# The third mixer's inverse: substitution on 16x16 blocks, the rest by products on TensorE

## The chip, the cores and the metric

The kernel runs on one core of a Trainium2 chip. The metric is the device time of one execution in microseconds. The profile is of one execution, and its times are in microseconds unless marked ns. Engines: PE is TensorE, DVE VectorE, ACT ScalarE, POOL GpSimd, SP SyncE, which issues most DMAs. A name such as `SPq` is an engine's queue of DMA issues.

## The reference

Two layers of a diffusion backbone, each with three mixers side by side (a gated linear attention, a windowed attention and an RWKV-7 time mixing), a merge through sigmoid gates, and a feed-forward part. The change is in the third mixer, which runs this recurrence in both directions of time:

```python
def rwkv7_scan(r, w, k, v, kk, a, s0, with_out):
    def step(S, inp):
        w_t, k_t, v_t, kk_t, a_t = inp[:5]
        sa = jnp.einsum('bhvk,bhk->bhv', S, kk_t)
        S = S * w_t[:, :, None, :] - sa[..., None] * (kk_t * a_t)[:, :, None, :] + v_t[..., None] * k_t[:, :, None, :]
        return S, jnp.einsum('bhvk,bhk->bhv', S, inp[5])
    s_fin, y = lax.scan(step, s0, xs)
```

Eight heads of 64 channels, 768 tokens, in fp32. Taken over a block of 32 tokens, the terms with `kk` make a unit triangular system of 32x32 for each head, whose inverse turns the block's inputs into its updates of the state.

## The kernel before

The class `Rwkv` has two lanes: f runs forward in time, b backward. Each takes six groups of 128 tokens, four blocks of 32 each. A group has two parts. Its **front** is `prep` (decay sums; the products `xp` of keys and updates, which a mask turns into the tile `X` on DVE, L1507; the products `bk` transposed by PE into `tp` and copied to `bkt` on ACT, L1518 and L1519) and then `inverse`. Its **chain** is four steps, one for each block: `yp` on PE (L1576, L1581), negated into `ysb` on ACT (L1586), `up` = inverse times `ysb` on PE (L1596), copied to `uv` on ACT (L1604), `sp` on PE, and the new state `sblk` on DVE (L1617); POOL scales the old state into `scf` or `scb` meanwhile (L1590). The output `op` (L1602, L1622) stands beside it.

`inverse` takes 32 triangular systems at once (4 pairs of heads x 2 heads x 4 blocks), four copies of each, so that 128 partitions hold 8 of the 32 rows each. The triangles go from `X` to DRAM (`d1`, two DMAs, L1530) and come back broadcast as `L` of 128 x 32 x 32 (L1532). `G` starts as an identity from DRAM (`gid`, on ACT's queue, L1537). 31 steps of substitution follow, each a product into `ftmp` (L1548) and a subtraction from `G` (L1549), in lane f on DVE and in lane b on POOL. `G` goes to DRAM (`d2`, four DMAs, L1553) and comes back as `TT` (L1555), which `up` reads.

The two lanes take turns, and before each half step of a chain two steps of the next group's front are issued. In layer 0 the fronts run one group ahead (`ahead`), in layer 1 two. In between, GEMM jobs of other parts fill PE: `px` and `pz` (three products of fp32 halves `hh`, `hl` with `wh`, `wl`; `wh` is made on ACT, L71, and `wl` on DVE, L72). In layer 0 they are spread by the number of turns, in layer 1 paced by the chain's hops. The order on each engine is set by the Tile scheduler from the program as written; every engine works its list in that order. The PSUM tag "a" with two buffers is shared by `xp`, `tp` and, later, `gp` and `ty`.

Of the kernel before, what the change touches and what calls it, by code (L numbers as in the profile page):

```python
# [1216 lines left out]
class Rwkv:  # L1217
# [43 lines left out]
    def open(self):  # L1261
# [13 lines left out]
        self.masks = ld("rmask", [128, 2, 64], I["rmask"])  # L1275
        self.smask = P.tile([128, 16, 34], F32, name="smask")
# [3 lines left out]
        for d in "fb":  # L1280
            self.sc[d] = P.tile([128, 4, 64], F32, name=f"sc{d}")
            t = P.tile([128, 4, 128], F32, name=f"sblk{d}")
            nc.gpsimd.memset(t, 0.0)
            self.sb[d] = t

# [236 lines left out]
    def inverse(self, d, g, later):  # L1522

        nc, T = self.nc, self.T
        d1 = self.D.tile([2, 16, 32, 32], F32, name="d1", tag="d1", bufs=3)
        d2 = self.D.tile([8, 4, 32, 32], F32, name="d2", tag="d2", bufs=3)
        X = self.hs[d, g]["X"]
        for q in range(2):
            r0 = 0 if q == 0 else 96
            nc.sync.dma_start(d1[q].rearrange("u j i -> j u i"), X[r0:r0 + 32].rearrange("j e w p i -> j (e w p) i")[:, :, 0:32])  # L1530
        L = T.tile([128, 32, 32], F32, name="L", tag="L", bufs=2)
        nc.sync.dma_start(L.rearrange("u j i -> u (j i)"), d1.rearrange("q u j i -> (q u) (j i)").unsqueeze(1).to_broadcast([32, 4, 1024]))  # L1532
# [3 lines left out]
        G = T.tile([128, 8, 32], F32, name="G", tag="G", bufs=2)  # L1536
        nc.scalar.dma_start(G, self.I["gid"])  # L1537
        tmp = T.tile([128, 128], F32, name="ftmp", tag="ftmp", bufs=2)
        eng = nc.vector if d == "f" else nc.gpsimd
        for n in range(31):  # L1540
            if d == "f":
                j, rows, cols = n, slice(0, n // 4 + 1), slice(n + 1, 32)
            else:
                j = 31 - n
                rows, cols = slice(j // 4, 8), slice(0, j)
            a, m = rows.stop - rows.start, cols.stop - cols.start
            t = tmp[:, 0:a * m].rearrange("q (a b) -> q a b", b=m)
            eng.tensor_tensor(out=t, in0=G[:, rows, j:j + 1].to_broadcast([128, a, m]), in1=L[:, j:j + 1, cols].to_broadcast([128, a, m]), op=ALU.mult)  # L1548
            eng.tensor_tensor(out=G[:, rows, cols], in0=G[:, rows, cols], in1=t, op=ALU.subtract)  # L1549
            if n % 8 == 7:  # L1550
                yield
        for s in range(4):
            nc.sync.dma_start(d2.rearrange("m p (a s) i -> s (m p) a i", s=4)[s], G[s::4])  # L1553
# [180 lines left out]
def _consts():  # L1734
    f = np.float32
# [145 lines left out]
```

## Time and profile before

| | |
|---|---|
| median of 3 runs (lowest, highest) | 3249.8 us (3247.38, 3262.34) |
| the profiled execution's own time | 3250.64 us |
| its span | 3248.8 us |
| PE busy | 2975.4 us, 92% of the span |
| DVE busy | 1735.5 us, 53% |
| ACT busy | 1126.6 us, 35% |
| POOL busy | 951.7 us, 29% |

The span is the part of the profiled execution between its first and its last instruction; 1.8 us of that execution lie around it. Busy time is an average over parts with different limits, and the third mixer's recurrence fills two stretches of the span: about 660 to 1100 us in layer 0 and 2340 to 2760 us in layer 1. Waits name the engine and line whose end let the waiting one go on. The granted clock is the share of full speed that TensorE was given.

### The profile page before, as it was taken

Reading aid. Unit: us, or ns where it says so; the run is one execution under the profiler, and the core shown is the slowest. Engines: PE = TensorE matmul, PEld = TensorE weight load, DVE = VectorE, ACT = ScalarE, POOL = GpSimd, SP = SyncE. Lnnn points to the kernel's source line nnn. Section 1 sums busy time; section 2 is a strip of 40 time slices with the busy share of each in tenths; the row PEclk is TensorE's granted clock in tenths of the full one; section 3 lists DMA queues with packets and bytes.
Section 4 is the critical chain, followed back from the end, with each engine's and each line's share of the span. In section 5 each row is a group of like instructions: output and inputs, shape, how many; then the busy total and the mean of one; then the engine's idle time right before and its main releaser. Section 6 shows DMA issues by size and latency. Waiting matters only on the chain. (4 is left out here: it accounts for less than half of the span.)

```text
span 3248.8 us, 62663 instructions
## 1 busy us (share of the span) xinstructions
PE 2975.4 (92%) x25760; PEld 2376.0 (73%) x25760; DVE 1735.5 (53%) x3336; ACT 1126.6 (35%) x2226; POOL 951.7 (29%) x1344
## 2 busy tenths in 40 slices
PE   6999999889999899999999899798877889899998
PEld 3777877676767788888888777576655556788887
DVE  3184666767757744222223454656667666543335
ACT  3154454433333323112122443553323333332223
POOL 3033212236655322101011212222256753220102
PEclk9999999898899999999999899899877889999999
DMA  7421222364455542443223222123555453523333
GB/s 293 157 77 59 94 82 108 133 191 126 122 151 164 185 156 103 163 147 120 65 65 93 93 77 92 57 81 120 170 148 144 127 159 124 177 72 98 93 102 117
DMA packets 271103, 398.33 MB, mean 123 GB/s; under 512 B 96352, under 2 KB 181088, under 8 KB 270816
## 3 DMA queue, kind: packets, MB, share of 16 engines
q1 hardware_dynamic: 243616, 360.76, 34.7%
q10 hardware_dynamic: 27200, 33.56, 3.1%
q8 instruction: 202, 3.31, 0.4%
q14 instruction: 85, 0.70, 0.1%
HBM read 320.33 MB, written 73.92 MB: 121 GB/s over the span
## 5 line engine op out<-in xcount | busy, mean ns | idle before, releaser
L50 PE MATMUL px<-hh,wh 128*128 128x512 f32 x1584 | 651.6, 412 | 26.4 <-ACT wh L71 18.9
L50 PE MATMUL px<-hh,wl 128*128 128x512 f32 x1584 | 645.0, 407 | 20.1 <-DVE wl L72 20.0
L50 PE MATMUL px<-hl,wh 128*128 128x512 f32 x1584 | 641.5, 405 | 10.1 <-POOL hl L302 8.9
L71 ACT ACTIVATE wh<-raw 128x1024 fp32r<-128x1024 f32 (+1 forms) x314 | 326.3, 1042 | 837.7 <-PE pz L50 408.3
L72 DVE TENSOR_TENSOR wl<-raw,wh 128x1024 fp32r<-128x1024 f32 (+1 forms) x314 | 400.4, 1276 | 357.6 <-ACT wh L71 324.1
L50 PEld LDWEIGHTS px<-hh,wh 128*128 128x128 f32 x1584 | 309.0, 195 | 120.1 <-issue 24.2
L50 PEld LDWEIGHTS px<-hh,wl 128*128 128x128 f32 x1584 | 308.4, 195 | 95.9 <-DVE wl L72 24.3
L50 PEld LDWEIGHTS px<-hl,wh 128*128 128x128 f32 x1584 | 308.5, 195 | 79.3 <-POOL hl L302 13.3
L673 POOL TENSOR_TENSOR al<-fs,ah 128x768 fp32r<-128x768 f32 (+1 forms) x44 | 85.0, 1931 | 726.3 <-ACT ah L672 726.3
L50 PE MATMUL pz<-hl,wh 128*128 128x256 f32 x872 | 252.8, 290 | 2.8 <-POOL hl L302 1.6
L50 PE MATMUL pz<-hh,wh 128*128 128x256 f32 x872 | 252.3, 291 | 1.5 <-DVE fs L663 1.4
L50 PE MATMUL pz<-hh,wl 128*128 128x256 f32 x872 | 251.3, 288 | 1.3 <-DVE wl L72 0.8
L50 PEld LDWEIGHTS pz<-hl,wh 128*128 128x128 f32 x872 | 170.3, 195 | 9.6 <-issue 2.4
L50 PEld LDWEIGHTS pz<-hh,wh 128*128 128x128 f32 x872 | 169.6, 195 | 9.8 <-issue 1.8
L50 PEld LDWEIGHTS pz<-hh,wl 128*128 128x128 f32 x872 | 170.0, 195 | 6.1 <-issue 4.0
L50 PE MATMUL px<-y,wh 128*128 128x512 f32 (+1 forms) x512 | 150.8, 383 | 25.7 <-ACT y L123 12.6
L1548 POOL TENSOR_TENSOR ftmp<-G,L 128x60 f32<-128x60 f32 (+24 forms) x372 | 136.0, 366 | 90.4 <-DMA TT<-d 24.2
L1549 POOL TENSOR_TENSOR G<-G,ftmp 128x60 f32<-128x60 f32 (+24 forms) x372 | 136.2, 366 | 27.2
L1548 DVE TENSOR_TENSOR ftmp<-G,L 128x60 f32<-128x60 f32 (+24 forms) x372 | 114.0, 306 | 52.4 <-DMA L<-d 24.8
L50 PEld LDWEIGHTS px<-y,wh 128*128 128x128 f32 x512 | 93.9, 206 | 44.1 <-ACT y L123 13.5
L1549 DVE TENSOR_TENSOR G<-G,ftmp 128x60 f32<-128x60 f32 (+24 forms) x372 | 114.2, 307 | 10.9
L231 POOL TENSOR_TENSOR sqa<-sqa,sq 128x256 f32<-128x256 f32 (+1 forms) x70 | 71.8, 1026 | 159.7 <-ACT sq L229 148.3
(444 smaller groups left out, 5962.5 us busy)
## 6 DMA issues: line engine op xcount, KB each, us to landing
raw<-win SPq DMA_DIRECT2D x114, 512.0 KB, 3.6
raw<-w SPq DMA_DIRECT2D x104, 512.0 KB, 3.5
araw<-wada SPq DMA_DIRECT2D x96, 512.0 KB, 5.2
raw<-w SPq DMA_DIRECT2D x48, 448.0 KB, 3.3
kr<-krd SPq DMA_DIRECT2D x24, 512.0 KB, 5.1
L<-d SPq DMA_DIRECT2D x24, 512.0 KB, 4.1
gs<-gat ACTq DMA_DIRECT2D x24, 384.0 KB, 2.6
raw<-wab SPq DMA_DIRECT2D x16, 512.0 KB, 4.3
```

The source lines that it names most:

```text
L50: return self.nc.tensor.matmul(out, lhsT=lhsT, rhs=rhs, start=start, stop=stop)
L71: nc.scalar.activation(h[:, :n], raw[:, :n], AF.Copy)
L72: nc.vector.tensor_tensor(out=lo[:, :n], in0=raw[:, :n], in1=h[:, :n].bitcast(F32), op=ALU.subtract)
L231: nc.gpsimd.tensor_tensor(out=acc[:, :n], in0=acc[:, :n], in1=sq[:, :n], op=ALU.add)
L673: nc.gpsimd.tensor_tensor(out=al, in0=s, in1=ah.bitcast(F32), op=ALU.subtract)
L1548: eng.tensor_tensor(out=t, in0=G[:, rows, j:j + 1].to_broadcast([128, a, m]), in1=L[:, j:j + 1, cols].to_broadcast([128, a, m]), op=ALU.mult)
L1549: eng.tensor_tensor(out=G[:, rows, cols], in0=G[:, rows, cols], in1=t, op=ALU.subtract)
```

## The change

`inverse` now inverts the two 16x16 blocks on the diagonal of each triangle by substitution: `d1` is written in four DMAs of 16x16 pieces, `L` is 128 x 16 x 16, `G` is 128 x 8 x 16 and starts as a copy by ACT from an identity kept in SBUF, and 15 steps (30 operations) follow instead of 31 (62). The results go into the diagonal blocks of `d2`, four tiles per layer that are zeroed when the layer's recurrence opens, and come back as `TT`. The off-diagonal block is made on PE: eight products `ep` transpose `TT` (copied by ACT into `E`), 32 products `qp` multiply it by `X` (copied by ACT into `Q`), 32 products `fp` multiply that by `TT`, and one DVE operation adds the result, with its sign and half chosen by the column `other`, to `TT`. `ep`, `qp` and `fp` use the PSUM tag "a". `inverse` has six points at which it yields, before five.

```diff
--- before.py
+++ after.py
@@ -1273,6 +1273,8 @@
         self.gnw = ld("gnw", [128, 128], I["gnw"][l])
         self.gnb = ld("gnb", [128, 128], I["gnb"][l])
         self.masks = ld("rmask", [128, 2, 64], I["rmask"])
+        self.gid = ld("rgid", [128, 8, 16], I["gid"])
+        self.other = ld("rother", [128, 2], I["other"])
         self.smask = P.tile([128, 16, 34], F32, name="smask")
         nc.vector.memset(self.smask, 1.0)
         nc.vector.memset(self.smask[:, :, 0:1], 0.0)
@@ -1282,6 +1284,13 @@
             t = P.tile([128, 4, 128], F32, name=f"sblk{d}")
             nc.gpsimd.memset(t, 0.0)
             self.sb[d] = t
+        zero = P.tile([128, 256], F32, name="zero")
+        nc.gpsimd.memset(zero, 0.0)
+        self.d2 = {d: [self.D.tile([8, 4, 32, 32], F32, name=f"d2{d}{i}") for i in range(2)] for d in "fb"}
+        self.turn = {"f": 0, "b": 0}
+        for d in "fb":
+            for t in self.d2[d]:
+                nc.sync.dma_start(t.rearrange("m p (x r) i -> (m p x) (r i)", x=4), zero)
 
     def close(self):
         self.ctx.close()
@@ -1521,38 +1530,69 @@
 
     def inverse(self, d, g, later):
 
-        nc, T = self.nc, self.T
-        d1 = self.D.tile([2, 16, 32, 32], F32, name="d1", tag="d1", bufs=3)
-        d2 = self.D.tile([8, 4, 32, 32], F32, name="d2", tag="d2", bufs=3)
+
+        nc, T, ps, K = self.nc, self.T, self.ps, self.K
+        d1 = self.D.tile([2, 2, 16, 16, 16], F32, name="d1", tag="d1", bufs=3)
+        d2 = self.d2[d][self.turn[d] % 2]
+        self.turn[d] += 1
         X = self.hs[d, g]["X"]
+        rows = (slice(0, 32), slice(96, 128))
         for q in range(2):
-            r0 = 0 if q == 0 else 96
-            nc.sync.dma_start(d1[q].rearrange("u j i -> j u i"), X[r0:r0 + 32].rearrange("j e w p i -> j (e w p) i")[:, :, 0:32])
-        L = T.tile([128, 32, 32], F32, name="L", tag="L", bufs=2)
-        nc.sync.dma_start(L.rearrange("u j i -> u (j i)"), d1.rearrange("q u j i -> (q u) (j i)").unsqueeze(1).to_broadcast([32, 4, 1024]))
+            for h in range(2):
+                r0 = rows[q].start + 16 * h
+                nc.sync.dma_start(d1[h, q].rearrange("u j i -> j u i"), X[r0:r0 + 16].rearrange("j e w p i -> j (e w p) i")[:, :, 16 * h:16 * h + 16])
+        L = T.tile([128, 16, 16], F32, name="L", tag="L", bufs=2)
+        nc.sync.dma_start(L.rearrange("u j i -> u (j i)"), d1.rearrange("h q u j i -> (h q u) (j i)").unsqueeze(1).to_broadcast([64, 2, 256]))
+        G = T.tile([128, 8, 16], F32, name="G", tag="G", bufs=2)
+        nc.scalar.copy(G, self.gid)
         yield
         if later is not None:
             self.load(d, later)
-        G = T.tile([128, 8, 32], F32, name="G", tag="G", bufs=2)
-        nc.scalar.dma_start(G, self.I["gid"])
-        tmp = T.tile([128, 128], F32, name="ftmp", tag="ftmp", bufs=2)
+        tmp = T.tile([128, 64], F32, name="ftmp", tag="ftmp", bufs=2)
         eng = nc.vector if d == "f" else nc.gpsimd
-        for n in range(31):
+        for n in range(15):
             if d == "f":
-                j, rows, cols = n, slice(0, n // 4 + 1), slice(n + 1, 32)
+                j, ra, cols = n, slice(0, n // 2 + 1), slice(n + 1, 16)
             else:
-                j = 31 - n
-                rows, cols = slice(j // 4, 8), slice(0, j)
-            a, m = rows.stop - rows.start, cols.stop - cols.start
+                j = 15 - n
+                ra, cols = slice(j // 2, 8), slice(0, j)
+            a, m = ra.stop - ra.start, cols.stop - cols.start
             t = tmp[:, 0:a * m].rearrange("q (a b) -> q a b", b=m)
-            eng.tensor_tensor(out=t, in0=G[:, rows, j:j + 1].to_broadcast([128, a, m]), in1=L[:, j:j + 1, cols].to_broadcast([128, a, m]), op=ALU.mult)
-            eng.tensor_tensor(out=G[:, rows, cols], in0=G[:, rows, cols], in1=t, op=ALU.subtract)
-            if n % 8 == 7:
+            eng.tensor_tensor(out=t, in0=G[:, ra, j:j + 1].to_broadcast([128, a, m]), in1=L[:, j:j + 1, cols].to_broadcast([128, a, m]), op=ALU.mult)
+            eng.tensor_tensor(out=G[:, ra, cols], in0=G[:, ra, cols], in1=t, op=ALU.subtract)
+            if n == 7:
                 yield
-        for s in range(4):
-            nc.sync.dma_start(d2.rearrange("m p (a s) i -> s (m p) a i", s=4)[s], G[s::4])
+        to = d2.rearrange("m p (h a s) i -> h s (m p) a i", h=2, s=2)
+        for h in range(2):
+            for s in range(2):
+                nc.sync.dma_start(to[h, s][:, :, 16 * h:16 * h + 16], G[64 * h + s:64 * h + 64:2])
         TT = self.hs[d, g]["TT"] = T.tile([128, 8, 32], F32, name="TT", tag="TT", bufs=4 if self.zout else 6)
         nc.sync.dma_start(TT, d2.rearrange("m p r i -> (p r) m i"))
+        yield
+        ep = ps.tile([128, 4, 128], F32, name="ep", tag="a", bufs=2)
+        for m in range(8):
+            nc.tensor.matmul(ep[rows[m // 4], m % 4, :], lhsT=TT[:, m, :], rhs=K.ident, start=True, stop=True, skip_group_check=True)
+        E = T.tile([128, 4, 128], F32, name="E", tag="E", bufs=2)
+        for r in rows:
+            nc.scalar.copy(E[r], ep[r])
+        yield
+        Q = T.tile([128, 2, 4, 32], F32, name="Q", tag="Q", bufs=2)
+        for q, r in enumerate(rows):
+            qp = ps.tile([128, 4, 32], F32, name="qp", tag="a", bufs=2)
+            for m in range(4):
+                for p in range(4):
+                    nc.tensor.matmul(qp[32 * p:32 * p + 32, m, :], lhsT=X[r, m // 2, m % 2, p, 0:32], rhs=E[r, m, 32 * p:32 * p + 32], start=True, stop=True, skip_group_check=True)
+            nc.scalar.copy(Q[:, q], qp)
+        yield
+        fp = ps.tile([128, 8, 16], F32, name="fp", tag="a", bufs=2)
+        c0 = 16 if d == "f" else 0
+        for m in range(8):
+            for p in range(4):
+                r = slice(32 * p, 32 * p + 32)
+                nc.tensor.matmul(fp[r, m, :], lhsT=Q[r, m // 4, m % 4, :], rhs=TT[r, m, c0:c0 + 16], start=True, stop=True, skip_group_check=True)
+        di = "fb".index(d)
+        o = TT[:, :, c0:c0 + 16]
+        nc.vector.scalar_tensor_tensor(out=o, in0=fp, scalar=self.other[:, di:di + 1], in1=o, op0=ALU.mult, op1=ALU.add)
         yield
 
     def chain(self, it):
@@ -1754,11 +1794,12 @@
     m[:, 0, :32], m[:, 0, 32:] = j < i, j <= i
     m[:, 1, :32], m[:, 1, 32:] = j > i, j >= i
     C["rmask"] = m
-    g = np.zeros((128, 8, 32), f)
-    for s_ in range(4):
+    g = np.zeros((128, 8, 16), f)
+    for s_ in range(2):
         for a in range(8):
-            g[s_::4, a, 4 * a + s_] = 1
+            g[s_::2, a, 2 * a + s_] = 1
     C["gid"] = g
+    C["other"] = np.stack([np.where(p % 32 < 16, -1.0, 0.0), np.where(p % 32 < 16, 0.0, -1.0)], 1).astype(f)
 
     T = np.arange(512)
     inv = 10000.0 ** (-np.arange(16, dtype=np.float32) / np.float32(16))
```

Line numbers shift: of the lines named above, L1507 becomes L1516, L1512 L1521, L1518 L1527, L1548 and L1549 become L1561 and L1562, L1576 L1616, L1596 L1636, L1602 and L1622 become L1642 and L1662, L1615 and L1617 become L1655 and L1657. Three places in the order, each of the kernel before and then of the changed one.

PE in layer 1, where the first `up` stands; before:

```order
L50 MATMUL xp_23686<-kr_23466,bk_23467 64x64 x2
L50 MATMUL xp_23687<-kr_23466,bk_23467 64x64 x2
L1596 MATMUL up_23659<-ysb_23628,TT_23313 32x64 x8
L50 MATMUL px_23865<-hh_2_18166,wh_23031 128x512
L50 MATMUL px_23865<-hl_2_18174,wh_23031 128x512
L50 MATMUL px_23865<-hh_2_18166,wl_23032 128x512
L50 MATMUL px_23865<-hh_3_18167,wh_23031 128x512
L50 MATMUL xp_23751<-kr_23491,bk_23492 64x64 x11
L50 MATMUL sp_23672<-uv_22837,bkt_23142 64x64 x8
L50 MATMUL xp_23752<-kr_23491,bk_23492 64x64 x3
L1596 MATMUL up_23724<-ysb_23648,TT_23333 32x64 x8
```

After, where `qp` and `fp` are the products of the first fronts of this layer:

```order
L1584 MATMUL qp_23968<-E_23934,X_23719 32x32 x16
L1584 MATMUL qp_23987<-E_23946,X_23756 32x32 x16
L1584 MATMUL qp_24005<-E_23946,X_23756 32x32 x16
L1592 MATMUL fp_24023<-TT_23903,Q_23949 32x16 x32
L1592 MATMUL fp_24057<-TT_23923,Q_23986 32x16 x32
L50 MATMUL xp_24108<-kr_23840,bk_23841 64x32 x16
L1636 MATMUL up_24519<-ysb_24488,TT_23903 32x64 x4
L50 MATMUL xp_24109<-kr_23840,bk_23841 64x32 x16
L50 MATMUL xp_24145<-kr_23863,bk_23864 64x32 x16
L50 MATMUL xp_24146<-kr_23863,bk_23864 64x32 x16
L1527 MATMUL tp_24185<-ident_61,bk_23841 128x128 x4
L1636 MATMUL up_24519<-ysb_24488,TT_23903 32x64 x4
```

The first `up` stood behind `xp` of a later front; now `qp` and `fp` of the inverse that it reads, `TT_23903`, stand right ahead of it.

PE in layer 0, in the second front, where `up` and `op` belong to a chain that runs meanwhile; before:

```order
L50 MATMUL sp_6977<-uv_6325,bkt_6548 64x64 x2
L1622 MATMUL op_6972<-uv_6325,X_6413 32x64 x5
L1596 MATMUL up_7038<-ysb_6892,TT_6859 32x64 x8
L1576 MATMUL yp_7113<-uv_6325,X_6413 32x64 x8
L50 MATMUL xp_7914<-kr_7222,bk_7223 64x64 x2
L50 MATMUL px_7627<-hh_0_131,wh_7343 128x512
L50 MATMUL px_7627<-hl_0_139,wh_7343 128x512
```

After, where `ep_7546` belongs to the front whose `X` is `X_7117`:

```order
L1636 MATMUL up_7367<-ysb_7244,TT_6731 32x64 x8
L1642 MATMUL op_7376<-sblkf_6312,kr_6328 32x128 x4
L1636 MATMUL up_7448<-ysb_7282,TT_6751 32x64 x8
L1574 MATMUL ep_7546<-ident_61,TT_7446 32x128 x8
L50 MATMUL px_7815<-hh_0_131,wh_7309 128x512
L50 MATMUL px_7815<-hl_0_139,wh_7309 128x512
L50 MATMUL pz_7840<-hh_0_131,wh_7309 128x256
L50 MATMUL pz_7840<-hl_0_139,wh_7309 128x256
L50 MATMUL sp_7385<-uv_6339,bkt_6562 64x64 x2
L1662 MATMUL op_7376<-uv_6339,X_6427 32x64
L50 MATMUL sp_7385<-uv_6339,bkt_6562 64x64 x2
```

Where `up` was followed by `yp`, `xp` of the next front and the GEMM products, `ep` now stands between `up` and the GEMM products, and it reads `TT_7446` of a front whose chain comes an iteration later.

DVE in layer 0, in the second front, where `X` and `bk` belong to a front and the `ftmp` and `G` rows to an inverse; before:

```order
L1548 TENSOR_TENSOR ftmp_6655<-G_6653,L_6579 128x60
L1507 TENSOR_TENSOR X_6999<-xp_7000,rmask_6302 128x512
L1507 TENSOR_TENSOR X_6999<-xp_7001,rmask_6302 128x512
L1512 TENSOR_TENSOR bk_6649<-bk_6649,pc_6877 128x1024
L1549 TENSOR_TENSOR G_6653<-G_6653,ftmp_6655 128x3x20
L1548 TENSOR_TENSOR ftmp_6655<-G_6653,L_6579 128x76
L1549 TENSOR_TENSOR G_6653<-G_6653,ftmp_6655 128x4x19
L1548 TENSOR_TENSOR ftmp_6655<-G_6653,L_6579 128x72
L1549 TENSOR_TENSOR G_6653<-G_6653,ftmp_6655 128x4x18
L1548 TENSOR_TENSOR ftmp_6655<-G_6653,L_6579 128x68
```

After:

```order
L1655 COPY sblkf_6312<-sp_7095 64x4x64 x2
L1516 TENSOR_TENSOR X_7117<-xp_7118,rmask_6302 128x512
L1516 TENSOR_TENSOR X_7117<-xp_7119,rmask_6302 128x512
L1521 TENSOR_TENSOR bk_6669<-bk_6669,pc_7055 128x1024
L1655 COPY sblkb_6315<-sp_7170 64x4x64 x2
L1561 TENSOR_TENSOR ftmp_7411<-G_7267,L_7265 128x15
L1562 TENSOR_TENSOR G_7267<-G_7267,ftmp_7411 128x15
L1561 TENSOR_TENSOR ftmp_7411<-G_7267,L_7265 128x14
L1562 TENSOR_TENSOR G_7267<-G_7267,ftmp_7411 128x14
L1561 TENSOR_TENSOR ftmp_7411<-G_7267,L_7265 128x26
L1562 TENSOR_TENSOR G_7267<-G_7267,ftmp_7411 128x2x13
L1561 TENSOR_TENSOR ftmp_7411<-G_7267,L_7265 128x24
```

Operations of 60 to 76 elements a row have given way to ones of 13 to 26, and the state `sblk` stands between them and `X`.

## Rows read from the trace of the kernel before

**Rows 1.** Stretches of the span: length, busy us (instructions) of each engine, granted clock, DMA share

```profile
core 0: us, PE busy (x) PEld busy (x) DVE busy (x) ACT busy (x) POOL busy (x), PEclk, DMA share, GB/s
660.00:1100.00 440.00, 402.86 (x5805) 309.11 (x5797) 315.42 (x722) 151.99 (x409) 242.25 (x491) 0.92 0.51 152
2340.00:2760.00 420.00, 350.43 (x4927) 247.02 (x4926) 278.51 (x666) 142.58 (x380) 230.99 (x486) 0.82 0.50 146
...
2660.00:2740.00 80.00, 78.70 (x1306) 52.44 (x1298) 43.07 (x87) 29.10 (x93) 36.19 (x51) 1.00 0.47 145
```

**Rows 2.** Waits of PE, 2344 to 2760 us: total us, times, longest us

```profile
PE px L50 <- DVE wl L72: 13.7, 7, 6.1
...
PE yp L1581 <- DVE sblkb L1617: 9.1, 5, 3.8
...
PE tp L1518 <- DVE X L1507: 6.2, 3, 2.9
PE tp L1518 <- POOL bk L1512: 5.4, 1, 5.4
```

**Rows 3.** Waits of PE, 660 to 1060 us

```profile
PE px L50 <- DVE wl L72: 5.9, 4, 3.8
PE yp L1581 <- DVE sblkf L1617: 4.6, 2, 3.2
PE yp L1581 <- DVE sblkb L1617: 4.4, 5, 2.3
```

**Rows 4.** Timeline of DVE: start us, us, operation [idle us before, what ended it]

```profile
2492.06 1.29 DVE L1507 TENSOR_TENSOR X<-xp,rmask 128x512 f32<-128x512 f32 x2
2498.93 0.19 DVE L1548 TENSOR_TENSOR ftmp<-G,L 128x31 f32<-128x31 f32 x1 [5.58 <-DMA G<-gid]
...
2502.81 1.21 DVE L72 TENSOR_TENSOR wl<-raw,wh 128x1024 fp32r<-128x1024 f32 x1
```

**Rows 5.** Timeline of PE, the px behind that wl

```profile
2504.07 0.80 PE L50 MATMUL px<-hh,wl 128*128 128x512 f32 x1 [3.54 <-DVE wl L72]
```

**Rows 6.** Whole span, operations with ftmp alone: busy us (instructions) of DVE, POOL

```profile
0.00:3249.00 3249.00, 228.24 (x744) 272.25 (x744) 0.94 0.38 123
```

**Rows 7.** Timeline of DVE, two short operations of the substitution

```profile
2369.64 0.18 DVE L1548 TENSOR_TENSOR ftmp<-G,L 128x30 f32<-128x30 f32 x1
2369.85 0.19 DVE L1549 TENSOR_TENSOR G<-G,ftmp 128x30 f32<-128x30 f32 x1
```

**Rows 8.** Timeline of POOL, the same

```profile
2424.77 0.24 POOL L1548 TENSOR_TENSOR ftmp<-G,L 128x29 f32<-128x29 f32 x1
2425.08 0.25 POOL L1549 TENSOR_TENSOR G<-G,ftmp 128x29 f32<-128x29 f32 x1
```

**Rows 9.** Timeline of PE, the first up of layer 1

```profile
2418.41 0.65 PE L1596 MATMUL up<-ysb,TT 32*32 32x64 f32 x16 [8.04 <-DMA TT<-d]
```

**Rows 10.** DMA issues, 2340 to 2760 us: KB each, median us to landing

```profile
L<-d SPq DMA_DIRECT2D x12, 512.0 KB, 3.9
...
d<-X SPq DMA_DIRECT2D x24, 64.0 KB, 3.2
d<-G SPq DMA_DIRECT2D x48, 32.0 KB, 2.7
TT<-d SPq DMA_DIRECT2D x12, 128.0 KB, 4.0
```

**Rows 11.** ACT's groups, 2340 to 2760 us: busy us, mean ns; idle us before

```profile
L1519 ACT COPY bkt<-tp 128x512 f32<-128x512 f32 x24 | 13.6, 588 | 21.8 <-PE tp L1518 21.6
L1586 ACT ACTIVATE ysb<-yp 128x128 f32<-128x128 f32 x48 | 13.3, 278 | 46.6 <-PE yp L1581 45.8 <-issue 0.4
```

**Rows 12.** Timeline of PE, bursts at the full clock

```profile
2674.50 0.43 PE L1596 MATMUL up<-ysb,TT 32*32 32x64 f32 x16
...
2679.02 0.43 PE L1581 MATMUL yp<-sblkf,kr 128*32 128x128 f32 x8
```

**Rows 13.** Timeline of PE, a burst of the first mixer

```profile
212.77 1.02 PE L50 MATMUL gsc<-gD,gD 64*32 64x32 f32 x96
```

## The prediction

> **What bounds the kernel now.** I read the table of stretches first, because the change touches only the third mixer and that mixer runs in two stretches: about 660 to 1100 us (layer 0) and 2340 to 2760 us (layer 1) [rows 1]. The reader should take three columns from it. TensorE (PE) is busy for 402.86 of 440 us in the first and 350.43 of 420 in the second, so it idles 37.1 and 69.6 us. VectorE (DVE) and GpSimd (POOL), which run the substitution, are busy about 315 and 242 us of 440: neither is the bound. And the granted clock is 0.92 and 0.82, against 1.00 in the 80 us at the end of layer 1 in which no front runs any more. What the clock takes is (1 - 0.92) x 440 = 35 us and (1 - 0.82) x 420 = 76 us. Beside the idle time that is one to one: a microsecond of idle PE here comes with about one more of a slower clock. So a wait of PE that goes, or comes, counts twice in the sums below.
>
> Next the waits of PE [rows 2, 3]: who keeps PE idle. In layer 1 the waits that the substitution can have a hand in are those for work that stands behind it in the queue of DVE or POOL: px for wl 13.7, yp for sblkb 9.1, tp for X 6.2, tp for bk 5.4, together 34.4 us. In layer 0 they are 5.9, 4.6 and 4.4, together 14.9. The sum is 49.3 us. One case in detail [rows 4, 5]: DVE finishes X at 2493.4, idles 5.58 us for the inverse of the f lane to start, runs its first substitution operations from 2498.93, and takes up wl only at 2502.81; PE's px then starts at 2504.07 after 3.54 us of idleness. Part of that is the queue, part the DMA ahead of it.
>
> **The change part by part.** *Substitution.* 62 operations of an inverse become 30, all of at most 36 elements a row. Now they take 228.24 us on DVE and 272.25 on POOL for 744 each [rows 6], or 19.0 and 22.7 us an inverse. Short ones follow each other after 0.21 us on DVE and 0.31 on POOL [rows 7, 8], so 30 of them take 6.3 and 9.3 us: two thirds of the work goes. If the 49.3 us of waits shrink by the same two thirds, that is 33 us, doubled for the clock 66. The bounds are 0 (the waits belong to the DMA ahead of the substitution, as the 5.58 us of [rows 4] do, or to a DVE that is still busy with wl) and 99, all of them twice. I take 66, as most of the 34.4 and 14.9 us are waits for short operations of DVE that stand among the substitution's.
>
> *Start of layer 1.* The first up waits 8.04 us for TT [rows 9]. A shorter substitution brings this TT forward, while the new products behind TT push it back: the first excerpt of the order has qp and fp directly ahead of that up, with a copy on ACT between the two and an addition on DVE behind them. Between 0 and 16 us with the clock; the substitution of POOL shrinks by 13.4 us and the new links are a few copies, so I take 16.
>
> *DMA and ACT.* L shrinks from 512 to 128 KB, the 128 KB of gid stay in SBUF, d1 is written in four pieces instead of two. The tables show 3.2 us for d1's write, 3.9 for L, 2.7 for d2's, 4.0 for TT [rows 10]; none is a matter of bandwidth that PE waits for. The shorter L may save a microsecond in the trip below, SP's two more issues may take it. Per layer there are four more writes of 128 KB as it opens, ahead of anything that PE needs. ACT gets one G copy, two E copies and two Q copies per inverse; at 588 ns for 128x512 and 278 for 128x128 [rows 11] that is 0.28 + 1.18 + 0.56 = 2.0 us, 48 us in all on an engine busy 152 of 440 us [rows 1]. I cost DMA and ACT at 0, within 10 either way; if ACT's room were gone, the 48 us would stand in front of ysb and uv, which the chain waits for.
>
> *New work on PE.* An inverse gets 8 ep products (128 columns), 32 qp (32 columns) and 32 fp (16 columns). In the trace a product in fp32 counts twice. 4 yp calls of 128 columns (x8) take 0.43 us, 8 up calls of 64 columns (x16) take 0.43, and 48 gsc calls of 32 columns (x96) take 1.02 [rows 12, 13]. So ep takes 0.7 to 0.9 us; qp takes 0.7 if it goes as gsc does, and up to 1.7 if each call costs what an up call does; fp the same. That makes 2.1 to 4.3 us, and with the ends of each burst, where PE changes tile, up to 4.6. I take 3.0, nearest to gsc, the only row with so few columns: 24 x 3.0 = 72 us, with bounds of 50 and 110. Idle time of PE is 8% of the one stretch and 17% of the other and can take in some of it; I count three quarters, 54 us, on the path (bounds 36 and 110).
>
> *The new wait.* Before, the first reader of TT on PE was up, in the next iteration of the chain or later. Now ep reads TT within the same front, and PE works in order: everything behind ep, the GEMM jobs and the other lane's chain, waits with it. The second excerpt shows ep_7546 with px and sp right behind it. Between the last xp of this front and that ep the order has 24 px, 24 pz, 16 tp and 100 products in fp32, so 264 instructions in the trace's count. At this stretch's rate, 440 us for 5805 [rows 1], they take 20.0 us. In that time X must be masked and moved (1.29 us) [rows 4], written to d1 and read as L (3.2 + 3.9), substituted (6.3, on POOL 9.3), written to d2 and read as TT (2.7 + 4.0): 21.4 us in the f lane and 24.4 in the b lane, with no other operation in between. PE comes 1.4 to 4.4 us too early. I take 3.5 for a pair of fronts, since DVE and POOL have other work in between and the two lanes' trips overlap. The first pair of each layer stands where PE waits anyway; 10 pairs x 3.5 x 2 (clock) = 70 us. Bounds: 0, if TT is there in time, and 10 x 8.04 x 2 = 161, if each is as long as the longest wait for TT that PE has now [rows 9]. The cause that keeps ep early is the PSUM tag that xp, tp, ep, qp and fp share, with two buffers.
>
> *The sum*, against the profiled execution's own 3250.6 us (the median of the runs, 3249.8, is 0.8 lower): 3250.6 - 66 - 16 + 54 + 70 = 3292.6, **3293 us**.
>
> **The rivals.** *Few columns are not cheaper.* If qp and fp cost per call what up does, the new work is the upper 110 us, three quarters of it 83: 3293 + 29 = 3322 us. For it: no row shows 16 columns. Against it: gsc's 48 calls in 1.02 us are 21 ns each, up's 8 in 0.43 are 54.
>
> The Trainium skill, "TensorEngine Tiling (Array Packing)", section Instruction Overhead, states this as a rule that speaks against the change: a product has an overhead of some 60 cycles, and one column costs as much as 60. By it qp and fp would be priced as up, and the time would be this rival's. The gsc row does not bear it out at 32 columns.
>
> *The wait at ep is long.* 8.04 us a pair: 3293 - 70 + 161 = 3384 us. For it: the trip has four DMAs in a row, and rows of single landings leave out the queue on SP. Against it: DVE and POOL are freer than before.
>
> *TT is there in time (faster).* If DVE and POOL, freed of two thirds of the substitution, bring TT ahead of ep, the wait is nothing; chain steps then shorten by what stood ahead of sblk and wl (86 of the 99 us) and PE's new work falls into idle time but for 40: 3250.6 - 86 - 16 + 40 = 3189 us. It decides at a trip of under 20 us. For it: both engines had the substitution as their largest item here; the trip's 21.4 us is only just over. Against it: PE was 92% busy in layer 0, so that there is little room for 36 us of products.
>
> *Even.* Relief of 50, waits of 1 us a pair, 40 of work: 3250.6 - 50 - 16 + 40 + 20 = 3245 us.
>
> **How the numbers follow.** The forecast (3265 to 3325 by half of its terms' bounds) has 0.40, few columns 0.08, the long wait 0.08, even 0.20, faster 0.24. A measurement of this kernel tells about 0.5%, 16 us, from no change. Faster is thus 0.24, same 0.20, slower 0.56. The range leaves out half of the long waits and the far end of the faster case, so it runs from 3190 to 3345 us.
>
> **What would show it.** Right: a wait of PE at ep for TT of a few us in most fronts; DVE and POOL some 150 us less busy each; the granted clock in both stretches no higher than 0.92 and 0.82; ep, qp and fp together near 72 us. Wrong: if ep waits for nothing, and the waits for wl, sblk and X shrink by more than half, the faster case holds; if those waits stay as they are, then they were never the substitution's, and the relief of 66 falls; if the bursts of qp and fp take 1.4 us each, few columns are not cheaper.

## The result, and the profile after

The changed kernel takes 3355.7 us (median of 4 runs, 3353.1 to 3363.5); the kernel before took 3251.6 in the runs beside it. The ratio is 1.031 (95% interval 1.029 to 1.034): 104 us slower. The forecast was 3293, slower by 43; its range ended at 3345.

First the stretches of the third mixer, each from its first `xp` to 5 us behind its last `up`. Columns: stretch, its length, busy time of PE, of its weight loads, of DVE, ACT and POOL with instructions, granted clock, DMA share, GB/s. The kernel before:

```profile
659.00:1086.00 427.00, 392.62 (x5724) 300.84 (x5723) 301.58 (x687) 147.75 (x402) 239.48 (x490) 0.92 0.50 148
2346.00:2752.00 406.00, 341.04 (x4888) 239.26 (x4886) 268.17 (x640) 135.74 (x369) 230.99 (x486) 0.83 0.49 144
```

The changed kernel:

```profile
656.00:1154.00 498.00, 443.45 (x7523) 343.07 (x7521) 231.93 (x511) 171.86 (x463) 167.95 (x299) 0.89 0.39 114
2414.00:2852.00 438.00, 385.76 (x6565) 275.89 (x6563) 204.66 (x450) 155.29 (x422) 156.91 (x294) 0.82 0.40 114
```

The two stretches grew by 71 and 32 us, which is the whole difference. DVE and POOL are less busy, as the change meant; PE's busy time grew by 51 and 45 us. The clock fell in the first stretch and stayed low in the second. Two sums over both stretches will be used below for every kernel: idle time of PE (length less busy), here 99 us before and 107 after, and an estimate of what the clock takes (1 less the clock, times the length), 103 before and 134 after.

The new products and the substitution, over the whole span of the changed kernel. The first three rows are those of `ep`, `qp` and `fp` (PE busy, PE's loads, then ACT's or DVE's operations on the tile), the last that of `ftmp` (DVE, POOL), to be read against [rows 6]:

```profile
0.00:3352.00 3352.00, 45.65 (x384) 35.83 (x384) 27.70 (x48) 0.93 0.35 115
0.00:3352.00 3352.00, 22.83 (x1536) 19.22 (x1536) 12.27 (x48) 0.93 0.35 115
0.00:3352.00 3352.00, 18.85 (x1536) 16.14 (x1536) 8.42 (x24) 0.93 0.35 115
0.00:3352.00 3352.00, 81.46 (x360) 120.38 (x360) 0.93 0.35 115
```

The products take 87 us of PE, where 72 were expected (the expectations of the experiments reckon with 80), and the substitution 81 and 120 us, where 76 and 112 were expected. PE's waits at `ep` in the first stretch (total us, times, longest):

```profile
PE ep L1574 <- DMA TT<-d2f: 3.2, 2, 1.7
PE ep L1574 <- DMA TT<-d2b: 2.9, 2, 2.7
PE ep L1574 <- ACT bkt L1528: 2.5, 1, 2.5
```

In the second stretch there are 3.7 us more. So PE waits about 10 us for TT at `ep`, where the forecast had 35. The wait of tp for X, of which [rows 2] has 6.2 us in layer 1, grew; in the first and the second stretch it is:

```profile
PE tp L1527 <- DVE X L1516: 11.9, 4, 5.5
...
PE tp L1527 <- DVE X L1516: 10.5, 4, 5.8
```

The wait of the first up for TT ([rows 9]) is gone. By these sums the 87 us of work on PE would be most of the 104. Whether that is so, the experiments ask.

### The profile page after: what moved, and what is told of

Its sections match the earlier page's. It is cut to its first block, busy times and chain, and to the rows that moved or that the text cites. A ratio compares the mean times of both kernels' runs of the same rounds, so it can differ in the third digit from the quotient of the medians.

```text
span 3351.3 us, 69027 instructions
## 1 busy us (share of the span) xinstructions
PE 3063.3 (91%) x29216; PEld 2449.2 (73%) x29216; DVE 1605.3 (48%) x2976; ACT 1172.6 (35%) x2346; POOL 802.3 (24%) x962
## 5 line engine op out<-in xcount | busy, mean ns | idle before, releaser
L50 PE MATMUL px<-y,wh 128*128 128x512 f32 (+1 forms) x512 | 159.0, 398 | 25.4 <-ACT y L123 11.1
L1630 POOL TENSOR_TENSOR scf<-sblkf,pc 64x256 f32<-64x256 f32 x92 | 63.2, 687 | 256.7 <-DVE sblkf L1657 230.4
L50 PE MATMUL px<-ah,wh 128*128 128x512 f32 x296 | 116.1, 393 | 0.0
L1644 ACT COPY uv<-up 32x128 f32<-32x128 f32 x384 | 98.6, 257 | 48.3 <-PE up L1636 40.6
L50 PE MATMUL px<-ah,wl 128*128 128x512 f32 x296 | 115.3, 390 | 0.0
L50 PE MATMUL px<-al,wh 128*128 128x512 f32 x296 | 115.3, 389 | 0.0
```

Of the source, the lines that this page charges most:

```text
L50: return self.nc.tensor.matmul(out, lhsT=lhsT, rhs=rhs, start=start, stop=stop)
L1630: nc.gpsimd.tensor_tensor(out=self.sc[d][rr], in0=S[rr, :, 64 * e:64 * e + 64], in1=pc[rr, :, cl:cl + 1].to_broadcast([64, 4, 64]), op=ALU ...
L1644: nc.scalar.copy(uv[ru, p].rearrange("q e v -> q (e v)"), up[32 * p:32 * p + 32, :])
```

## The experiments

Runs of the kernel before drift by up to 7 us from chip to chip, so each run is given as the ratio to the kernel before on the same chip, with its interval, and as its own median. Differences between runs are differences of these ratios, times 3252 us; most of them are uncertain by some 10 to 15 us.

### The relief alone, the products alone, and less work in `ep`

e1 takes the products out. The off-diagonal half of the inverse is left out of it:

```diff
-        ep = ps.tile(...)      # and all up to the addition into TT
```

> The changed kernel without the off-diagonal part: ep, E, qp, Q, fp and the addition into TT are left out, so the off-diagonal half of each inverse stays zero. Theory A (the time is the work of ep, qp and fp on PE, 80 us in the trace of the changed kernel, all of it on the path and dearer by the clock, and the shorter substitution relieved nothing): 3245 to 3262 us. Theory B (the shorter substitution does relieve the chain by the 66 to 82 us of the prediction, and the products then cost over 170): 3165 to 3190 us.

Ratio 0.985 (0.982 to 0.988), 3209.6 us: 48 us faster than before, which lies between both theories.

e2 adds the three bursts to the kernel before, behind its own TT, unread (`nc.tensor.matmul` of the same counts and tiles, `qp` with the identity for E, `fp` with TT for Q); the front gets three more steps by it:

> The kernel before, with its 31-step substitution untouched, and the three bursts ep, qp and fp issued behind TT in the front with the same counts, tiles and PSUM tag; nobody reads them, and no copies or additions are added. Theory A: the products are the whole story, 80 to 105 us on top: 3330 to 3357 us. Theory B: the products cost over 160: over 3410 us. A third theory, C (not the work, but the order of the front costs: copies E and Q, the addition, everything between ep and fp): under 3300 us.

Ratio 1.058 (1.054 to 1.062), 3447.4 us: 189 us slower, more than theory A allowed and as theory B had it. Here the wait of the forecast does appear. The waits of PE over the whole span of e2:

```profile
PE tp L1518 <- DVE X L1507: 38.4, 10, 8.5
...
PE ep L1560 <- DMA TT<-d: 30.5, 10, 10.7
```

With 31 steps of substitution ahead of TT, `ep` waits 30 us; with 15 it waits 10. So the wait that the forecast put on `ep` exists, but with the shorter substitution it is small.

e3 changes the order of `ep`, e5 makes it of two transposes:

```diff
-        for m in range(8):
+        for m in (0, 4, 1, 5, 2, 6, 3, 7):                       # e3
```

```diff
-            nc.tensor.matmul(ep[rows[m // 4], m % 4, :], lhsT=TT[:, m, :], rhs=K.ident, ...)
+            nc.tensor.transpose(ep[:, q, :], TT[:, 4*q:4*q+4, :], K.ident)   # e5, q = 0, 1
```

> The changed kernel with the eight ep products issued in the order 0, 4, 1, 5, 2, 6, 3, 7, so that neighbours write the two different groups of 32 rows in turn. If neighbours in different groups of columns of the array overlap (as yp and up do, whose four groups alternate), the burst of ep falls from 1.8 to some 0.9 us, and theory A gives 24 x 0.9 = 21 us less, with the clock up to 30: 3325 to 3335 us. Theory C: no change, 3350 to 3360 us.

> The changed kernel with ep made by two 128x128 transposes instead of eight products of 32x128, and E copied by eight ACT copies of 32x128 (0.26 us each) instead of two of 32x512 (0.58 each). PE work of an inverse falls by some 1.5 us, ACT work grows by 0.9. Theory A: 24 x 1.5 = 36 us less, with the clock up to 50: 3305 to 3320 us. Theory C (copies and order between ep and fp cost, not the work): 3355 to 3375 us.

e3: 1.036 (1.033 to 1.040), 3376.4 us. e5: 1.027 (1.024 to 1.031), 3345.4 us. In e3 `ep` fell from 45.65 us to 33.7 and the kernel got no faster: its ratio is 17 us above the changed kernel's, at the edge of the noise. In e5 it fell by 34 us, to two transposes of 12 us in all, and 12 us came back instead of 36 to 50. The stretches of e5 and its waits at `ep`:

```profile
658.00:1152.00 494.00, 441.54 (x7361) 339.55 (x7360) 239.94 (x515) 183.27 (x536) 169.85 (x299) 0.86 0.41 116
2406.00:2852.00 446.00, 385.83 (x6428) 271.81 (x6426) 203.86 (x462) 170.08 (x503) 158.26 (x294) 0.78 0.39 111
```

```profile
PE ep L1574 <- DMA TT<-d2b: 12.1, 9, 3.5
...
PE ep L1574 <- DMA TT<-d2f: 9.3, 3, 5.1
```

PE's busy time fell by only 2 us although 34 us of work were taken out: the clock went to 0.86 and 0.78, what it takes went from 134 to 167 us, and the rest of the work was busy for longer. The wait at `ep` doubled, to 21 us. Theory A, that PE's time alone is the price, falls.

### Where `ep` stands, and the work without its links

e6 puts four empty steps (`yield`) ahead of `ep`. e8 is e1 with the same three bursts at the same steps, reading the identity and X, read by nobody. e10 makes E by one DVE transpose of 32x32 blocks, with X brought into the matching layout by DMA; e11 adds three empty steps to it:

```diff
+        for _ in range(4):                                       # e6; 3 in e11
+            yield
-        ep = ...; E = two ACT copies                             # e10, e11
+        nc.vector.transpose(E, TT)
```

> The changed kernel with four empty steps of the front between the read of TT and ep, so that ep stands two half steps of the chain later; no operation is added. By the first four runs the products cost 146 us for 80 us of work. Theory W (the rest comes from the front now passing through PE's queue: the order puts ep where TT only just arrives, and the chain's operations are laid around it): 25 to 60 us less, 3295 to 3330 us. Theory K (the rest is the clock, which answers the bursts themselves, wherever they stand): 3345 to 3365 us.

> The kernel of e1 (no off-diagonal part) plus the same three bursts of products at the same steps of the front, with the same counts, tiles and PSUM tag, but multiplying the identity and X instead of TT, E and Q, and read by nobody: the work without the links. e1 took 3209.6 us. Theory W: the work alone, 60 to 85 us: 3270 to 3295 us. Theory K: the bursts with their clock, near the changed kernel: 3330 to 3360 us.

> The changed kernel with E made by one transpose of 32x32 blocks on DVE instead of eight ep products and two ACT copies; X is brought into the matching layout (32 partitions for each pair of heads) by two more DMA writes and one read per inverse, and Q is copied in one piece. PE loses the 43.6 us of ep and the front loses two changes of engine. Theory W: the links get shorter by some 3 us a front, 24 x 3 with what the work gives: 3270 to 3310 us. Theory K: fewer bursts, so less low clock: 3270 to 3300 us as well; if neither, as in e5, about 3340 us.

> e10 with three empty steps of the front ahead of the transpose. Theory W: 25 to 50 us below e10, and if the products then cost no more than the 49 us that the shorter substitution gives, as fast as the kernel before: 3235 to 3275 us. Theory K: as e10.

e6: 1.037 (1.034 to 1.040), 18 us slower than the changed kernel's ratio. e8: 1.025 (1.023 to 1.027), 3331.7 us. e10: 1.027 (1.025 to 1.029), 14 us below the changed kernel with no `ep` on PE at all. e11: 1.031 (1.028 to 1.033). So a later `ep` gains nothing; but it still waits 10.0 us for TT in e6 (7.2 and 2.8 us in its list of waits), so that e6 doesn't tell what an `ep` without a wait would be worth. e8 tells more: the bursts without any link to TT already cost 128 us over e1, and the links add only 0.64%, 21 us. Theory W, that the links and the place of `ep` are the price, falls.

### Which burst costs

e9 is e1 with three empty steps in the products' place, to part the number of steps from the work. e13 keeps of e8 only `ep`, e14 only `qp` and `fp`. e15 is the kernel before with one part of the change, the identity for G kept in SBUF (in bf16, with a shorter `ftmp` to make room):

```diff
+        for _ in range(3):                                       # e9, in e1
+            yield
-        nc.scalar.dma_start(G, self.I["gid"])                    # e15, in the kernel before
+        nc.scalar.copy(G, self.gid)
```

> The kernel of e1 (no off-diagonal part, nothing in its place) with three empty steps of the front where the products' steps were, so that its front has 11 steps as the changed kernel's has. It separates the number of steps, by which the fillers and the chain are dealt out, from the work. If the work of the products is the cause of the 122 us between e1 and e8: within 12 us of e1, 3198 to 3222 us. If it is the dealing: 3280 to 3330 us.

> The kernel of e8 with the eight ep products alone, qp and fp left out, the steps of the front kept: 43 us of PE work. If the price goes by work, 122 x 43/80 = 66 us above e1: 3268 to 3285 us. If it goes by the number of bursts or of products (8 of 72), 15 to 35 us above e1: 3225 to 3245 us.

> The kernel of e8 with qp and fp alone, ep left out: 37 us of PE work. If the price goes by work, 122 x 37/80 = 56 us above e1: 3258 to 3275 us. If it goes by the number of bursts or of products (64 of 72), 85 to 110 us above e1: 3295 to 3320 us.

> The kernel before with one part of the change alone: the start value of G is a copy by ACT from SBUF instead of a DMA of 128 KB on ACT's queue. DVE's and POOL's idle time ahead of the first operation of an inverse that ended with this DMA was 16.8 and 14.2 us. If e1's gain over the kernel before comes from there, 20 to 45 us less: 3205 to 3232 us. If it comes from the fewer steps: no change, 3240 to 3262 us.

e9: 0.990 (0.988 to 0.993), 3223.2 us. e13: 0.9996 (0.998 to 1.001), 3253.4. e14: 1.020 (1.018 to 1.022), 3316.1. e15: 1.002 (1.001 to 1.003), 3261.4. So the shorter substitution gives 32 us where the front has the changed kernel's number of steps, and some 16 of e1's 48 came from the shorter front. In e15 the identity's DMA alone gives no gain. Over e9, which has the same steps, `ep` costs 31 us for its 36 us of PE; `qp` and `fp` cost 97 us for their 56; all three together (e8) cost 112 us for 98, so the two parts don't quite add up. The stretches of e9, e14 and e8:

```profile
663.00:1109.00 446.00, 405.55 (x5790) 310.58 (x5788) 227.45 (x499) 153.07 (x415) 170.81 (x299) 0.88 0.45 129
2366.00:2727.00 361.00, 321.43 (x4867) 225.31 (x4865) 201.49 (x443) 136.30 (x377) 162.72 (x294) 0.88 0.48 137
```

```profile
662.00:1152.00 490.00, 431.80 (x7326) 336.37 (x7324) 228.79 (x500) 152.03 (x415) 171.15 (x299) 0.84 0.41 118
2407.00:2820.00 413.00, 354.73 (x6370) 255.69 (x6368) 196.96 (x438) 135.41 (x374) 153.56 (x294) 0.82 0.42 120
```

```profile
658.00:1154.00 496.00, 449.69 (x7524) 353.51 (x7523) 230.12 (x500) 152.16 (x415) 170.02 (x299) 0.86 0.41 117
2410.00:2833.00 423.00, 373.63 (x6562) 271.71 (x6560) 197.23 (x438) 136.14 (x374) 154.72 (x294) 0.84 0.41 117
```

From e9 to e14 idle time goes from 80 us to 117 and the clock's share from 97 to 153. The new idle time stands where PE waits for the chain's own results (op for `ys`, yp and sp for the state, sp for `uv`, up for `ysb`): 19 us in the two stretches of e9, 64 in those of e14. In the first stretch of e9 the two largest of these waits are:

```profile
PE yp L1598 <- DVE sblkb L1634: 3.3, 2, 2.4
PE op L1619 <- ACT ys L1641: 3.0, 2, 2.7
```

and the three largest in that of e14:

```profile
PE op L1630 <- ACT ys L1652: 18.5, 6, 4.9
PE yp L1609 <- DVE sblkb L1645: 10.6, 5, 4.9
PE sp L50 <- ACT uv L1632: 6.3, 2, 3.9
```

A place where one sees it, the timeline of PE in e14 (start, us, operation, idle time before):

```profile
748.19 0.65 PE L1630 MATMUL op<-sblkb,kr 128*32 128x128 f32 x8 [4.70 <-ACT ys L1652]
...
749.12 1.12 PE L50 MATMUL sp<-uv,bkt 64*64 64x64 f32 x16
...
751.48 0.42 PE L1577 MATMUL qp<-ident,X 32*32 32x32 f32 x16
753.45 0.65 PE L1609 MATMUL yp<-sblkb,kr 128*32 128x128 f32 x8 [1.56 <-DVE sblkb L1645]
754.04 0.66 PE L1577 MATMUL qp<-ident,X 32*32 32x32 f32 x37
...
755.08 0.66 PE L1630 MATMUL op<-sblkf,kr 128*32 128x128 f32 x8
755.66 0.60 PE L1583 MATMUL fp<-ident 32*32 32x16 f32 x26
756.20 1.12 PE L50 MATMUL sp<-uv,bkt 64*64 64x64 f32 x16
```

and the stretch around it:

```profile
744.00:759.00 15.00, 9.25 (x264) 6.39 (x264) 9.95 (x12) 4.69 (x13) 13.17 (x24) 0.50 0.30 83
```

In 15 us PE is busy for 9, at half the clock throughout, and there is not one `px` or `pz`: where a GEMM product could cover the wait for ys or sblkb, pieces of `qp` and `fp` of half a microsecond stand. Counting the GEMM products (`px`, `pz`) in PE's order between one state of lane f and the next, steps 2 to 9 of layer 0:

| kernel | GEMM products in each chain step |
|---|---|
| e9 | 44, 48, 17, 36, 44, 47, 4, 63 |
| e14 | 0, 65, 37, 40, 0, 67, 27, 52 |

The changed kernel itself doesn't look like e14 here. Counted in its trace, the same steps have 17, 51, 34, 45, 28, 41, 20 and 52 GEMM products, and its waits for the chain's results are 23 us. Its idle time over e9 lies elsewhere: at `ep` for TT (10 us), ahead of `fp` (9) and at tp for X (4). So e14 shows what the narrow bursts do by themselves, not where the changed kernel loses the same time.

### Dealing the bursts out

That gave theory S: the order bunches the GEMM fillers around the bursts. e18 is e14 with `qp` in four steps of 8 products and `fp` in two of 16; e16, e19 and e20 do the same to the changed kernel, e5 and e10:

```diff
             for m in range(4):
+                if m == 2 or m == 0 and q:
+                    yield
```

> The kernel of e14 (no off-diagonal part, qp and fp unlinked) with qp issued in four parts of 8 products and fp in two of 16, each part a step of the front of its own; counts and work are the same. In the order the chain steps of layer 0 that hold the bursts had 0 GEMM products beside them in e14 and now have some 45. Theory S (the place of the fillers): back to the price of the work, 20 to 40 us above e9's 3223: 3243 to 3265 us. Theory K (the bursts themselves): as e14, 3305 to 3325 us.

> The changed kernel, whole, with qp in four steps of 8 products and fp in two of 16. Theory S: 30 to 60 us less than the changed kernel's 3355.7: 3295 to 3325 us. Theory K: no change, 3345 to 3365 us.

> e5 (ep as two transposes, eight ACT copies) with qp and fp dealt out as in e16. Theory S: PE's saved work now counts: 25 to 40 us below e16, 3260 to 3295 us. Theory K: as e5, 3335 to 3355 us.

> e10 (E by one transpose of 32x32 blocks on DVE, no ep on PE) with qp in four steps of 8 and fp in two of 16. Theory S: the work that is left is 37 us, and the substitution's gain is 36 to 49: 3245 to 3285 us, near the kernel before. Theory K: as e10, 3330 to 3350 us.

e18: 1.030 (1.026 to 1.034), 3355.1 us, 31 us slower than e14. e16: 1.032 (1.030 to 1.033), as the changed kernel. e19: 1.036 (1.033 to 1.039). e20: 1.039 (1.037 to 1.041). The steps of e18 have 45, 46, 0, 53, 45, 46, 0, 54 GEMM products, nearly as even as e9's, and it is slower. Dealing out also adds four steps to the front, but three empty ones cost only some 16 us between e1 and e9, and theory S had e18 at 3265 us or less. Theory S in this form falls.

### Number or time

e21 puts four products of the form of `ep` at `qp`'s step and four at `fp`'s, e22 the same 64 narrow products in bf16:

```diff
-                    nc.tensor.matmul(qp[...], lhsT=X[...], rhs=K.ident[r, 0:32], ...)     # 32 of them
+            nc.tensor.matmul(w[...], lhsT=K.ident[:, 0:32], rhs=K.ident, ...)             # e21: 4
+                    nc.tensor.matmul(qp[...], lhsT=self.idb[r, 0:32], rhs=self.idb[r, 0:32], ...)  # e22: 32
```

> The kernel of e14 (no off-diagonal part) with four unlinked products of the ep form (128 rows by 32 columns of weights, 128 moving columns, 0.11 us each record) at each of the two steps where qp's 32 and fp's 32 stood: 24 x 1.8 = 43 us of PE work where e14 had 37, with 8 products instead of 64. Theory N (the number and narrowness of the products is what costs, through the order laid around them): 3240 to 3262 us, 20 to 40 above e9. Theory T (PE time at these two steps costs 2.5 times itself, whatever form it has): 3305 to 3335 us.

> The kernel of e14 with the 64 unlinked products of qp and fp in bf16, on a copy of the identity in bf16: same number, shapes, tiles and steps, less time each on PE (one pass instead of two records). In the order the GEMM products are bunched around them much as in e14 (steps of 0, 9 and 5 products beside ones of 52 to 65). Theory N: as e14 or a little less, 3280 to 3318 us. Theory T: the price falls with the time, to half or less: 3235 to 3268 us.

e21: 0.997 (0.995 to 0.998), 3242.6 us. e22: 1.010 (1.008 to 1.012), 3283.4. PE's time on `qp` and on `fp` over the whole span, in e21 and then in e22:

```profile
0.00:3400.00 3400.00, 14.62 (x192) 9.80 (x192) 0.94 0.36 113
0.00:3400.00 3400.00, 18.23 (x192) 12.03 (x192) 0.94 0.36 113
```

```profile
0.00:3400.00 3400.00, 14.01 (x768) 0.93 0.37 113
0.00:3400.00 3400.00, 14.34 (x768) 0.93 0.37 113
```

At the same steps, 33 us of PE in 8 products an inverse cost 21 us over e9, and 28 us of PE in 64 products cost 64. The stretches of e21 and of e22:

```profile
664.00:1110.00 446.00, 412.85 (x5985) 318.50 (x5984) 233.83 (x500) 153.51 (x416) 172.59 (x299) 0.90 0.45 129
2367.00:2746.00 379.00, 338.20 (x5057) 238.30 (x5056) 197.02 (x443) 136.69 (x376) 160.43 (x294) 0.88 0.46 130
```

```profile
660.00:1138.00 478.00, 416.39 (x6563) 323.15 (x6561) 234.12 (x500) 151.55 (x415) 172.18 (x299) 0.85 0.43 121
2394.00:2783.00 389.00, 345.99 (x5636) 243.91 (x5634) 202.76 (x444) 137.29 (x377) 157.10 (x294) 0.82 0.45 127
```

| | us over e9 | PE busy on the bursts | idle | waits for the chain | clock |
|---|---|---|---|---|---|
| e9, none | 0 | 0 | 80 | 19 | 97 |
| e13, 8 `ep` | 31 | 36 | 89 | 40 | 91 |
| e21, 8 wide for `qp`, `fp` | 21 | 33 | 74 | 25 | 90 |
| e22, 64 narrow, bf16 | 64 | 28 | 105 | 43 | 142 |
| e14, 64 narrow, fp32 | 97 | 56 | 117 | 64 | 153 |
| e8, all 72, fp32 | 112 | 98 | 96 | 49 | 137 |

Eight wide products cost somewhat less than their time, and idle time and the clock's share stay within 10 us of e9's. The 64 narrow ones come with more idle time and a lower clock, and cost more than their own time, even where they take less of PE than the wide ones. That is shown; number and width were changed together, so it isn't shown which of the two counts. How the narrow products do it is not settled. The order around the narrow bursts is another one (e22's steps have 0, 65, 37, 42, 9, 56, 27, 54 GEMM products, e21's 44, 48, 16, 36, 47, 34, 30, 43), which fits a scheduler that takes 64 products for a long piece of work; but e18 has even steps and is slow. It may be the order within a step, between up and sp, the narrow products' own effect on the clock, or the buffers of the PSUM tag "a", of which an inverse takes three in e14 and e22, two in e21 and one in e13. PE's waits for the release of such a buffer (by `bkt` or `tsq`) are small, 4 us in e14 and 11 in e22 against 3 in e21, but the buffers may also shape the order. No run here parts these.

No run is a version that beats the kernel before: those that are as fast or faster leave the off-diagonal part out. e21 suggests what such a version would need, a few wide products instead of 64, but that form of the off-diagonal part wasn't tried.

## Why the prediction was wrong

It had the sign, and the size fell short by 61 us: the time lies outside its range. The step that failed is the price of the new work on PE, 54 us in the forecast and 112 in the runs; the relief was overrated too, and a wait at `ep` that was overrated in the other direction hid part of both. The runs give -32 (e9), +112 (e8 over e9) and +21 (the changed kernel over e8), together 101; the forecast had -82, +54 and +70, together 42. That the sign came out and the miss wasn't larger owes something to luck: with 21 us for the wait, the other terms as they were would have come to 3244 us, no change. By its own steps:

- *Substitution*, -66, and *start of layer 1*, -16. The cut in the operations' time came as forecast (81 and 120 us left). The relief was 48 us in e1 and 32 in e9, which has the front's 11 steps, against the 82 of the two terms. Of the waits that made up the 49.3 us, those of px for wl fell in e9 from 19.6 us to 12.1 and those of yp for the state from 18.1 to 10.9, by two fifths and not by two thirds, and tp for X, 6.2 us in the sum, is 17.9. So a good part of them was not the substitution's. The rows of e9, first stretch and then second:

```profile
PE tp L1527 <- DVE X L1516: 11.8, 4, 8.1
...
PE px L50 <- DVE wl L72: 4.4, 4, 1.9
...
PE px L50 <- DVE wl L72: 7.7, 5, 5.5
PE yp L1598 <- DVE sblkb L1634: 7.6, 2, 5.0
PE tp L1527 <- DVE X L1516: 6.1, 2, 4.4
```

  The first up's wait for TT went from 8.04 us to 3.1 in e9 and to nothing in the changed kernel.
- *New work on PE*, 54. This is the step that failed most, in both its factors. The work was 72 us in the forecast and is 87 in the changed kernel and 98 in e8. The burst of `ep` was priced at 0.7 to 0.9 us from yp's row; 45.65 us for 24 make 1.9, and 1.5 at the full clock. yp's four calls write four different groups of 32 rows, `ep`'s neighbours write the same one; in e3, where two groups alternate, the time falls to 33.7 us. `qp` and `fp` were priced nearly right (0.7 each, 0.95 and 0.79 found). The larger mistake was the share of the work that is on the path, "three quarters": the unlinked bursts together cost 3.5% over e9 (e8), 112 us for 98 of work. `ep` costs close to its time, `qp` and `fp` 97 us for the 56 that they take in e14. Why the narrow ones cost more than their time stays open.
- *The wait at ep*, 70. The wait is there, 10 us instead of 35, and e2, where the trip is longer, has 30. Both sides of the sum were too short, so that the difference stayed small: PE was to reach `ep` 20 us behind X and TT to be there after 21.4 or 24.4. In layer 0 of the changed kernel, behind the first pair, `ep` starts 23 to 33 us after the end of its front's X, and in the three longer of its waits for TT there the trip took 23, 30 and 30 us. All links together, with the copies, are 21 us.
- *Twice for the clock.* From idle time and clock before, one to one, the forecast doubled each wait. Between before and after idle time grew by 7 us, the clock's share by 30, and in e5 the clock's share grew by another 34 us with 6 more of idle time. The clock has to be its own term here.
- *DMA and ACT at 0.* Not contradicted: e15 shows no gain from taking out the identity's DMA (1.002), and e5, with ACT's work raised, is no slower than the changed kernel.
- *Few columns are not cheaper*, the rival with 0.08. A burst of `qp` (32 columns) takes 0.75 us in the changed kernel and one of `fp` (16 columns) 0.72:

```profile
847.29 0.75 PE L1584 MATMUL qp<-E,X 32*32 32x32 f32 x64
...
848.94 0.72 PE L1592 MATMUL fp<-TT,Q 32*32 32x16 f32 x64
```

  That is 23 ns a call for both, so half the columns saved nothing, though 64 columns of up took 54 ns [rows 12]. The Trainium skill, "TensorEngine Tiling (Array Packing)", section Instruction Overhead, says that a product of one column has the same latency as one of 60. In the spacing of these bursts the trace agrees between 32 and 16 columns; between 64 and 32 it doesn't. The rival's time of 3322 us was nearer than the forecast, but its reason, `qp` and `fp` priced as up, was not what happened.

The chance of 0.08 for anything beyond 3345 rested on one long wait. That relief and work could both fall short in the same direction (relief 50 us less, work 58 us more) was left out of the range.

## What to carry to other kernels

New work on PE in a stretch that waits for a chain isn't priced by its time alone: here 33 us in 8 wide products cost 21 us and 28 us in 64 narrow ones cost 64. Before trading vector operations for many small products, add the same products unread to the kernel at the place where they would stand, and see what they cost; and take the operation out with nothing in its place, to see the most that its removal can give (here 48 us, for 299 us of busy time saved on DVE and POOL, which were not the bound).

## What the runs showed of the hardware

With work taken out of `ep`, the granted clock was lower. e3 and e5 took 12 us and 34 us out of `ep`; the clock of the two stretches went from 0.89 and 0.82 to 0.84 and 0.79 (e3, over its own stretches) and to 0.86 and 0.78 (e5), and nothing or a third of the gain was left. What made it lower is not shown: in e5 PE also waits 11 us longer at `ep`. Products into the same 32 output rows follow each other more slowly than ones that alternate between two groups. One burst of `ep` at a granted clock of 1.00, in the changed kernel and then in e3:

```profile
742.24 1.50 PE L1574 MATMUL ep<-ident,TT 128*32 128x128 f32 x16 [1.55 <-DMA TT<-d2f]
```

```profile
746.62 1.07 PE L1574 MATMUL ep<-ident,TT 128*32 128x128 f32 x16 [1.63 <-DMA TT<-d2f]
```

All 24 bursts take 45.65 us against 33.7; the rows of `ep` in e3, for its two stretches, are:

```profile
661.00:1170.00 509.00, 16.23 (x192) 11.65 (x192) 13.84 (x24) 0.84 0.40 112
2426.00:2875.00 449.00, 17.47 (x192) 12.76 (x192) 13.82 (x24) 0.79 0.39 110
```
